# Reciprocal roots on GpSimd and one key split for both head pairs in a fused two-branch attention layer

## The chip, the cores and the metric

One core of one Trainium2 chip runs the kernel. The metric is the device time of one execution in microseconds. The core has five engines with a queue of instructions each: TensorE (PE, with its weight loads PEld beside it), VectorE (DVE), ScalarE (ACT), GpSimd (POOL) and SyncE (SP), which only issues DMAs here. An engine starts its instructions strictly in the order of its queue; semaphores order the engines among each other.

## The reference

Two request groups of 2048 tokens (`x_prompt`, `x_sample`), 1024 wide, pass one encoder layer with shared weights:

```python
h = rms_norm(x, norm_w)
q_a, k_a, v_a, g_a, q_b, k_b, v_b, g_b = split(h @ w_in)       # 512|128|128|512 and 4 x 512
q_a = partial_rope(rms_norm(q_a, q_norm_a)); k_a likewise      # per head of 64
o_a = windowed_gqa_sink(q_a, k_a, v_a, sink_a) * silu(g_a)     # 8 q heads, 2 kv heads, +-128 tokens
q_b = rms_norm(q_b, q_norm_b); k_b = rms_norm(k_b, k_norm_b)
o_b = neighbourhood_attn(q_b, k_b, v_b, rpb_b) * silu(g_b)     # 8 heads, 8 x 16 window on a 32 x 64 grid
x = x + concat(o_a, o_b) @ w_out
x = x + (p @ w_ple) * sigmoid(x @ w_ple_gate)
rms_norm(v, g) = v * rsqrt(mean(v * v) + 1e-6) * g
```

Every `rms_norm` needs a reciprocal root: one for each token, one for each head of q and of k of each token. The scores of a head are products of a normalized query and a normalized key, times `q_norm * k_norm / 8`, a factor for each of the 64 dimensions; it does not matter for the result on which of the two it is put.

## The kernel before

**Arithmetic.** Matrix products in float32 are made of three products of parts: a value is split into a high part (a copy rounded to the matmul's type, `fp32r`) and a low part (the value minus the high part), and high x high, high x low and low x high are summed. The high part is mostly a copy on ScalarE, the low part a subtraction on VectorE behind it (on GpSimd for the input x). So a tile's `project` (the helper that yields one matmul after another) is 8 x 3 = 24 matmuls of 128x128 by 512 columns (256 for `pk`).

**Stages.** `emit` writes the whole program, tile by tile, a tile being 128 tokens. The *start* (0 to about 50 us) loads and splits the first weights. The *first stage* (to about 745 us) handles branch A: 2 x 16 tiles, for each tile the projections `pk` (keys and values), `pq` and `pg` (`proj_a`), and the attention of the tile before (`unit_a`, twice, one for each kv head). The *second stage* (about 800 to 1870 us) handles branch B: two halves of four heads each, 2 x 16 tiles in each half, so 64 tiles, with the projections `pqk` and `pvg` (`proj_b`) and the attention (`unit_b`). Between the halves the weights are changed (about 1240 to 1275 us). The *last stage* (from about 1900 us) multiplies by `w_out` and the gate weights; there is no root and no key of branch B in it.

**What sets the order.** TensorE's order is fixed by hand: `mm` and `tr` (L211, L215) go through `pinned`, which ties each matmul or transpose to the one before. The tables `PLAN_A` and `PLAN_B` say at which point of the running projection which piece of an attention unit (`sc` scores, `pt` transposed exponentials, `po` output, `fin` the end of the unit, `prep` the split of the next queries) is emitted. On the other engines a scheduler sorts the instructions; those wrapped in `P` or `keep_in_program_order` keep the order of the program among themselves. Tile pools with few buffers (for example `bufs=2` for `kt`, 3 for `p_t`) tie an instruction to the last reader of the buffer.

**The root.** `rsqrt` (L135 to L145) makes y = 1/sqrt(v) on VectorE: an integer shift (L138), a subtraction from the constant 0x5F3759DF (L140), and three Newton steps of three instructions (L143 to L145): 11 instructions on a tile of 128 rows by n. It is called
- in `roots()` of `proj_a` with n = 3 (two heads of k and the token), once for each tile of the first stage; the scaled keys `kt` and their partial rotation on GpSimd (`rope`, L451 to L454) follow, and later `keys_a`, which splits the transposed keys into `ks_a` (L415, L418);
- at the end of `pq` in `proj_a` with n = 8 (eight heads of q); the multiply to `q` (L492) and a `rope` follow;
- in `proj_b` with n = 8 (four heads of q and four of k): `vrb` (L673) is the mean square, `yb` the root, and L679 multiplies it into `kb` (keys) and `qg` (queries);
- in `stats_b` with n = 16, twice, for the tokens of the second stage.

**Keys and queries of the second stage.** `keys_b` (L636) transposes the keys `kb` of a tile into the PSUM tile `pktb` (heads in pairs i, the two heads e of a pair in the two halves of the partitions) and splits them into `ks_b`: for each i and e one scaled copy on ScalarE (L645) and one scaled subtraction on VectorE (L646), 64 partitions by 128 elements, written in a scattered order (row of the grid, column). `wk[:, 1:2]`, the factor `q_norm * k_norm / 8`, is the scale. `prep_b` (L709) transposes the queries into `pqtb` and splits them without a scale: for each e a copy on ScalarE (L718), a subtraction on VectorE (L719), and a copy on GpSimd to the other half of the partitions (L721).

**Around it.** `softmax` (L227) is one VectorE instruction that adds the mask or bias to the scores and gives the row's maximum `mx`; `exps` negates the maximum (`nm`, L238 or L241), makes the exponentials on ScalarE (`s`, L243), and the denominators (L252 to L254); `pr` (L605) is the low part of the transposed exponentials of branch A; `otb` (L791) and `o_tb` (L798) are the unit's output; `split_w` (L157 to L164) splits a weight (`wx`, `wa`, `wb`); `split` (L307, L308) splits the input x.

Of the kernel before, what the change touches and what calls it, by code (L numbers as in the profile page):

```python
# [10 lines left out]

F32 = mybir.dt.float32
F32R = mybir.dt.float32r
I32 = mybir.dt.int32
AF = mybir.ActivationFunctionType
ALU = mybir.AluOpType
AX = mybir.AxisListType
# [3 lines left out]
NT = SEQ // 128  # L21
# [77 lines left out]
def emit(ctx, tc, io):  # L99
    nc = tc.nc  # L100
# [31 lines left out]
    ob_d = [dram.tile([4, 128, 4, 4, 128], F32, tag=f"ob_d{s}", name=f"ob_d{s}") for s in range(2)]  # L132
    ms_d = dram.tile([2 * SEQ], F32, tag="ms_d", name="ms_d")

    def rsqrt(pool, v, y, n, tag):  # L135
        i2 = pool.tile([128, n], I32, tag=tag + "i", name=tag + "i")
        a = pool.tile([128, n], F32, tag=tag + "a", name=tag + "a")
        nc.vector.tensor_scalar(out=i2, in0=v.bitcast(I32), scalar1=1, scalar2=None,  # L138
                                op0=ALU.logical_shift_right)
        nc.vector.tensor_scalar(out=y.bitcast(I32), in0=i2, scalar1=-1, scalar2=0x5F3759DF,  # L140
                                op0=ALU.mult, op1=ALU.add)
        for _ in range(3):
            nc.vector.scalar_tensor_tensor(out=a, in0=y, scalar=-0.5, in1=y, op0=ALU.mult, op1=ALU.mult)  # L143
            nc.vector.tensor_tensor(out=a, in0=a, in1=v, op=ALU.mult)
            nc.vector.scalar_tensor_tensor(out=y, in0=a, scalar=1.5, in1=y, op0=ALU.add, op1=ALU.mult)  # L145

    copies = []

# [272 lines left out]
    def proj_a(f):  # L421
# [35 lines left out]
        def roots():  # L457

            P(nc.vector.tensor_scalar(out=vr[:, 8:10], in0=ssq[:, 8:10], scalar1=1.0 / HD, scalar2=ee,
                                      op0=ALU.mult, op1=ALU.add))  # L460
            nc.vector.tensor_scalar(out=vr[:, 10:11], in0=ms, scalar1=EPS, scalar2=None, op0=ALU.add)
            rsqrt(ap, vr[:, 8:11], y[:, 8:11], 3, "rqk")
            nc.vector.tensor_scalar_mul(y[:, 11:12], y[:, 10:11], 0.5)
            nc.vector.tensor_tensor(out=kt[:, 0:2, :], in0=pk[:, 0:128].rearrange("p (h d) -> p h d", d=HD),
                                    in1=y[:, 8:10].unsqueeze(2).broadcast_to([128, 2, HD]), op=ALU.mult)
            rope(kt[:, 0:2, :], 2, 1)
# [4 lines left out]
        for i, c in enumerate(project(pq, xr, lambda k, b: w_q[k][:, b, :], 215)):  # L471
# [11 lines left out]
            if i == ka:  # L483
# [3 lines left out]
        nc.vector.tensor_reduce(out=ssq[:, 0:8], in_=sq.rearrange("p (h d) -> p h d", d=HD), op=ALU.add, axis=AX.X)  # L487
        nc.vector.tensor_scalar(out=vr[:, 0:8], in0=ssq[:, 0:8], scalar1=1.0 / HD, scalar2=ee,
                                op0=ALU.mult, op1=ALU.add)
        rsqrt(ap, vr[:, 0:8], y[:, 0:8], 8, "rqa")  # L490
        q = ap.tile([128, 8, HD], F32, tag="qg", name="q", bufs=6)
        nc.vector.tensor_tensor(out=q, in0=pq.rearrange("p (h d) -> p h d", d=HD),  # L492
                                in1=y[:, 0:8].unsqueeze(2).broadcast_to([128, 8, HD]), op=ALU.mult)
# [63 lines left out]
    def stats_b(s):  # L557
        c = slice(NT * s, NT * s + NT)
        tc.keep_in_program_order(nc.vector.tensor_scalar(out=ep_b[:, c], in0=ms_b[:, c], scalar1=EPS,
                                                         scalar2=EPS * EPS, op0=ALU.mult, op1=ALU.add))  # L560
        nc.vector.tensor_scalar(out=ms_b[:, c], in0=ms_b[:, c], scalar1=EPS, scalar2=None, op0=ALU.add)
        rsqrt(ap, ms_b[:, c], rs_b[:, c], NT, "rsb")
        nc.vector.tensor_scalar_mul(hr_b[:, c], rs_b[:, c], 0.5)

    qrest = {}
# [70 lines left out]
    def keys_b(kt, b, cb):  # L636
        pkt = ptile([128, 2, 16, 8], "ms", "pktb")
        for i in range(2):
            tr(pkt[:, i].rearrange("p c r -> p (c r)"), kt[:, 2 * i:2 * i + 2, :].rearrange("p h d -> p (h d)"))
        for i in range(2):  # L640
            for e in range(2):
                a, z = 64 * e, 64 - 64 * e
                hi, lo = (ks_b[i][p:p + 64, 8 * b:8 * b + 8, e, 16 * cb:16 * cb + 16].rearrange("p r c -> p c r")
                          for p in (a, z))
                nc.scalar.activation(hi, pkt[a:a + 64, i], AF.Copy, scale=wk[a:a + 64, 1:2])  # L645
                nc.vector.scalar_tensor_tensor(out=lo, in0=pkt[a:a + 64, i], scalar=wk[a:a + 64, 1:2],  # L646
                                               in1=hi.bitcast(F32), op0=ALU.mult, op1=ALU.subtract)

    def proj_b(f):
        half, st = divmod(f - 2 * NT, 2 * NT)  # L650
        s, j = divmod(st, NT)
        b, cb = divmod(j, 4)
        if f < 2 * NT + 8:
            regroup_next()
        if not ks_b:
            ks_b.extend(big([128, 32, 2, 64], F32R, f"ks_b{i}") for i in range(2))
        w_qk, w_vg = w_b[half]
        xr = xt.pop(f)
        pk = ptile([128, 512], "pj", "pqk")
        for i, c in enumerate(project(pk, xr, lambda k, b: ready("wa", k, w_qk)[:, b, :], 215)):  # L660
            at = i + 24 if f in last else i
            if i == PD and f == 2 * NT + 9:
                stats_b(1)
            if at in HX:
                split(f + 1, HX[at])
            yield c
        sq = ap.tile([128, 512], F32, tag="sq", name="sqb", bufs=2)
        nc.scalar.activation(sq, pk, AF.Square)
        ssq = ap.tile([128, 8], F32, tag="ssq", name="ssqb", bufs=3)
        nc.vector.tensor_reduce(out=ssq, in_=sq.rearrange("p (h d) -> p h d", d=HD), op=ALU.add, axis=AX.X)  # L670
        vr = ap.tile([128, 8], F32, tag="vr", name="vrb", bufs=2)
        y = ap.tile([128, 8], F32, tag="y", name="yb", bufs=4)
        nc.vector.tensor_scalar(out=vr, in0=ssq, scalar1=1.0 / HD, scalar2=ep_b[:, st:st + 1],  # L673
                                op0=ALU.mult, op1=ALU.add)
        rsqrt(ap, vr, y, 8, "rqb")
        qg = ap.tile([128, 2, 4, HD], F32, tag="qg", name="qg", bufs=6)
        kt = ap.tile([128, 4, HD], F32, tag="kt", name="kb", bufs=2)
        for dst, c in ((kt, 4), (qg[:, 0], 0)):
            nc.vector.tensor_tensor(out=dst, in0=pk[:, 64 * c:64 * c + 256].rearrange("p (h d) -> p h d", d=HD),  # L679
                                    in1=y[:, c:c + 4].unsqueeze(2).broadcast_to([128, 4, HD]), op=ALU.mult)  # L680
        yield 0, False
        pv = ptile([128, 512], "pj", "pvg")
        for i, c in enumerate(project(pv, xr, lambda k, b: ready("wb", k, w_vg)[:, b, :], 215)):
            if i + 24 in HX and f not in last:
                split(f + 1, HX[i + 24])
            yield c
            if i == (KB if f not in last else 10):
                if f < 2 * NT + 2:
                    pending.append((kt, b, cb))
                else:  # L690
                    keys_b(kt, b, cb)
        v = ap.tile([128, 4, 2, HD], F32R, tag="sq", name="vb", bufs=2)
        vp = pv[:, 0:256].rearrange("p (h d) -> p h d", d=HD)
        nc.scalar.activation(v[:, :, 0, :], vp, AF.Copy, scale=rs_b[:, st:st + 1])
        nc.vector.scalar_tensor_tensor(out=v[:, :, 1, :], in0=vp, scalar=rs_b[:, st:st + 1],
                                       in1=v[:, :, 0, :].bitcast(F32), op0=ALU.mult, op1=ALU.subtract)
        for w, (c0, ncol) in COL_WIN.items():
            lo, hi = max(c0, 16 * cb), min(c0 + ncol, 16 * cb + 16)
            if lo < hi:
                nc.sync.dma_start(v_d[half, s, w][8 * b:8 * b + 8, lo - c0:hi - c0].rearrange("r c h a d -> c r (h a d)"),  # L700
                                  v[8 * (lo - 16 * cb):8 * (hi - 16 * cb)].bitcast(F32).rearrange("p h a d -> p (h a d)"))
        gs = qg[:, 1].rearrange("p h d -> p (h d)")
        nc.scalar.activation(gs, pv[:, 256:512], AF.Tanh, scale=hr_b[:, st:st + 1])
        nc.vector.scalar_tensor_tensor(out=gs, in0=gs, scalar=1.0, in1=pv[:, 256:512], op0=ALU.add, op1=ALU.mult)
        held[f] = qg[:, 0], gs
        next(combining, None)
        yield 0, False

    def prep_b(f):  # L709
# [5 lines left out]
        q1, q2 = [q1[:, e] for e in range(2)], [q2s[f % 2][:, e, :256] for e in range(2)]  # L715
        for e in range(2):
            a, z = 64 * e, 64 - 64 * e
            nc.scalar.copy(q1[e][a:a + 64], pqt[a:a + 64])  # L718
            nc.vector.tensor_tensor(out=q2[e][a:a + 64], in0=pqt[a:a + 64], in1=q1[e][a:a + 64].bitcast(F32),  # L719
                                    op=ALU.subtract)  # L720
            nc.gpsimd.tensor_copy(q1[e][z:z + 64], q1[e][a:a + 64])  # L721
        return q1, q2

# [2 lines left out]
    def unit_b(f):  # L726
# [25 lines left out]
        def sc(h):  # L752
            ps = ptile([128, 512], "sc", "scb")
            for j, q in enumerate(qs[f]):
                mm(ps[:, :n].rearrange("p (r c) -> p r c", c=ncol), q[h % 2][:, 128 * (h // 2):128 * (h // 2) + 128],
                   ks_b[h // 2][:, r0:r0 + nr, h % 2, c0:c0 + ncol], j == 0, j == 1)
            softmax(h, ps, n, bias[:, h, :n], sm)
            if h == 3:
                got["ex"] = exps(sm, n, hr_b[:, st:st + 1], gs)
# [490 lines left out]
```

## Time and profile before

| what | value |
|---|---|
| runs | 2526.88, 2527.05, 2529.97 us (median 2527.05) |
| profiled execution | 2525.68 us; its span in the trace 2523.8 us |
| mean clock granted to TensorE | 0.996 of full speed |
| instructions | 41360 |
| busy PE, DVE, ACT, POOL | 2478.9, 1948.5, 1445.0, 582.5 us |
| DMA | 405.40 MB, mean 161 GB/s |
| chain that ended last | PE 86%, DVE 6%, DMA 3%, ACT 3% of the span |

The span is the time from the first to the last recorded instruction of the profiled execution; the execution's own time is somewhat longer. The busy time of an engine is the sum over its instructions; a matmul's end is modelled, and a weight load (PEld) runs beside the matmuls. The rows in the prediction come from these views: the page's first line and its busy line; a table by stretches (stretch, its length, then busy time with the number of instructions for PE, PEld, VectorE, ScalarE and GpSimd, then TensorE's granted clock, the mean busy share of the DMA engines and GB/s); groups of instructions (line, engine, operation, output <- inputs, shape, count | busy time in us, mean ns of one | idle time ahead of them and who ended it); a list of waits (who waits <- who ended the wait: sum in us, how many, the longest); and the timeline (start in us, duration in us, engine, line, operation, output <- inputs, shape, and in brackets a wait with its length and who ended it).

### The profile page before, as it was taken

To read this page: it belongs to the slowest core of one execution; us is meant where nothing else is said; L and a number is where in the kernel's file an instruction comes from. 1 tells how busy PE (TensorE), PEld (TensorE's weight loads), DVE (VectorE), ACT (ScalarE), POOL (GpSimd) and SP (SyncE) were. 2 spreads that over 40 slices of the span, in tenths; PEclk is the share of its full clock that TensorE was granted. 3 is DMA by queue.
4 is the path that set the end of the run, shared out by engine and by line. 5 is a ranking of instruction groups with operands and counts; after the bars stand their busy time and mean duration, and the time that the engine had idled before them with its cause. 6 is when DMAs were issued, how large, how long until landed. Compare 5 with 4: busy or idle time off the path is not lost.

```text
span 2523.8 us, 41360 instructions
## 1 busy us (share of the span) xinstructions
PE 2478.9 (98%) x12912; PEld 2090.0 (83%) x12912; DVE 1948.5 (77%) x5860; ACT 1445.0 (57%) x3469; POOL 582.5 (23%) x873
## 2 busy tenths in 40 slices
PE   8999999999989999999999999999999999999998
PEld 7888888888877888888788888888787888888887
DVE  7888888888887777787888777787746655687776
ACT  6666666666665566666666666666864222354433
POOL 3333233323323333333333333332110000000000
PEclk9999999999999999999999999999999999999999
DMA  5333332211143555555755655455867455756764
GB/s 200 98 102 109 108 88 95 64 53 62 57 101 121 167 171 177 183 166 167 235 160 180 191 160 168 147 158 185 267 230 265 160 181 171 266 176 221 235 228 154
DMA packets 236044, 405.40 MB, mean 161 GB/s; under 512 B 30864, under 2 KB 85264, under 8 KB 230416
## 3 DMA queue, kind: packets, MB, share of 16 engines
q1 hardware_dynamic: 235824, 402.75, 50.0%
q8 instruction: 103, 1.69, 0.3%
q14 instruction: 117, 0.96, 0.1%
HBM read 297.79 MB, written 122.70 MB: 167 GB/s over the span
## 4 chain that ended last, share of the span: by engine, by line
PE 86%; DVE 6%; DMA 3%; ACT 3%; issue 1%; POOL 0%; SPq 0%; DVEq 0%; ACTq 0%; POOLq 0%
PE pqk L212 13%; PE pvg L212 13%; PE acca L1082 12%; PE accc L1082 9%; PE pq L212 6%; PE pg L212 6%; PE scb L212 3%; PE ptb L215 3%; PE pob L212 3%; PE sc L212 3%; PE pk L212 3%; PE po L212 3%; PE pt L215 3%; PE pple L212 3%; ACT s L243 1%
## 5 line engine op out<-in xcount | busy, mean ns | idle before, releaser
L243 ACT ACTIVATE s<-s,nm 128x384 f32<-128x384 f32 (+4 forms) x512 | 307.3, 601 | 341.9 <-DVE nm L238 213.9
L212 PE MATMUL pvg<-wb,xr 128*128 128x512 f32 x1536 | 462.0, 408 | 0.0
L212 PE MATMUL pqk<-wa,xr 128*128 128x512 f32 x1536 | 444.7, 412 | 0.0
L212 PEld LDWEIGHTS pqk<-wa,xr 128*128 128x128 f32 x1536 | 267.7, 190 | 37.7
L212 PEld LDWEIGHTS pvg<-wb,xr 128*128 128x128 f32 x1536 | 268.4, 190 | 31.5
L308 POOL TENSOR_TENSOR xr<-stx,xr 128x512 fp32r<-128x512 f32 x190 | 245.1, 1297 | 187.0 <-ACT xr L307 180.4
L1064 ACT CAST opd<-raw 128x512 fp32r<-128x512 f32 x224 | 131.2, 619 | 261.8 <-PE acca L1082 112.8
L1065 DVE TENSOR_TENSOR opd<-raw,opd 128x512 fp32r<-128x512 f32 x224 | 146.3, 685 | 111.8 <-ACT opd L1064 111.8
L212 PE MATMUL pg<-wb,xr 128*128 128x512 f32 x768 | 231.8, 409 | 0.0
L212 PE MATMUL pq<-wa,xr 128*128 128x512 f32 x768 | 219.9, 400 | 2.2 <-DVE wa L160 1.6
L1082 PE MATMUL accc<-opd,wb 128*128 128x512 f32 x768 | 177.0, 389 | 1.9 <-DVE r L1126 1.9
L1082 PE MATMUL acca<-opd,wa 128*128 128x512 f32 x768 | 175.9, 389 | 0.4 <-DVE opd L1065 0.4
L1082 PE MATMUL acca<-opd,s 128*128 128x512 f32 x768 | 175.8, 389 | 0.2 <-DVE opd L1065 0.2
L798 POOL TENSOR_TENSOR o_tb<-otb 128x256 f32<-128x256 f32 x64 | 48.1, 751 | 547.2 <-DVE otb L791 466.8
L1082 PEld LDWEIGHTS accc<-opd,wb 128*128 128x128 f32 x768 | 144.1, 188 | 32.2 <-DVE r L1126 2.3
L1082 PEld LDWEIGHTS acca<-opd,wa 128*128 128x128 f32 x768 | 144.0, 188 | 30.9 <-DVE opd L1065 0.9
L1082 PEld LDWEIGHTS acca<-opd,s 128*128 128x128 f32 x768 | 144.0, 188 | 30.7 <-DVE opd L1065 0.9
L212 PEld LDWEIGHTS pq<-wa,xr 128*128 128x128 f32 x768 | 139.1, 188 | 25.5 <-DVE wa L160 3.3
L212 PEld LDWEIGHTS pob<-p_t,vw 128*128 128x128 f32 (+2 forms) x832 | 133.0, 190 | 30.9 <-DVE p_t L772 6.4
L227 DVE CUSTOM_DVE_ANT_0 s<-scb,bias 128x288 f32<-128x288 f32 (+3 forms) x256 | 141.3, 553 | 18.8 <-PE scb L212 15.8
L212 PEld LDWEIGHTS pg<-wb,xr 128*128 128x128 f32 x768 | 137.8, 189 | 20.4
L646 DVE SCALAR_TENSOR_TENSOR ks_b<-pktb,wk,ks_b 64x128 fp32r<-64x128 f32 x256 | 115.1, 450 | 43.9 <-ACT ks_b L645 33.4
(170 smaller groups left out, 5256.0 us busy)
## 6 DMA issues: line engine op xcount, KB each, us to landing
stx<-x_b SPq DMA_DIRECT2D x128, 256.0 KB
vw<-v_d SPq DMA_DIRECT2D x112, 256.0 KB
stx<-x_a SPq DMA_DIRECT2D x64, 256.0 KB
stn<-x_n SPq DMA_DIRECT2D x64, 256.0 KB
v_d<-vb SPq DMA_DIRECT2D x64, 256.0 KB
ple_d<-ev SPq DMA_DIRECT2D x64, 256.0 KB
xres<-x_r SPq DMA_DIRECT2D x64, 256.0 KB
x_d<-r SPq DMA_DIRECT2D x64, 256.0 KB
```

The lines of the kernel that those rows point to most:

```text
L212: pinned(nc.tensor.matmul(out, lhsT, rhs, start=start, stop=stop))
L215: pinned(nc.tensor.transpose(out, in_, eye))
L227: nc.vector.tensor_tensor_reduce(out=s[:, :n], in0=ps[:, :n], in1=bias, scale=1.0, scalar=-3.0e38, op0=ALU.add, op1=ALU.max, accum_out=sm[ ...
L243: ex = nc.scalar.activation(ss[i][:, :n], ss[i][:, :n], AF.Exp, bias=nm[:, i:i + 1], accum_out=den[:, i:i + 1])
L308: low.tensor_tensor(out=lo, in0=raw, in1=hi.bitcast(F32), op=ALU.subtract)
L646: nc.vector.scalar_tensor_tensor(out=lo, in0=pkt[a:a + 64, i], scalar=wk[a:a + 64, 1:2], in1=hi.bitcast(F32), op0=ALU.mult, op1=ALU.subtract)
L798: nc.gpsimd.tensor_tensor(out=o_t, in0=got["ot"][:, :, 0], in1=got["ot"][:, :, 1], op=ALU.add)
L1064: P(nc.scalar.copy(hi, v))
L1065: P(nc.vector.tensor_tensor(out=lo, in0=v, in1=hi.bitcast(F32), op=ALU.subtract))
L1082: pinned(nc.tensor.matmul(ps, w[k][:, a, c:c + 128], o[:, b], start=i in (0, 1, 4) and k == 0 and j == 0, stop=k == 3 and j == 2, skip_gro ...
```

## The change

`rsqrt` becomes one GpSimd instruction: v to the power of a constant tile that holds -0.5, on the same 128 rows by n. The eleven VectorE instructions and their two scratch tiles go. In `keys_b` the loop over the head pairs i goes: `ks_b` is indexed by the half of the partitions e first and by the pair i inside, so that one copy and one subtraction, 64 partitions by 256 elements, cover both pairs. The scale `wk` leaves the keys; the queries' split in `prep_b` gets it instead, with as many instructions as before. `unit_b` reads `ks_b` by the new indices.

```diff
-    def rsqrt(pool, v, y, n, tag):
-        i2 = pool.tile([128, n], I32, tag=tag + "i", name=tag + "i")
-        a = pool.tile([128, n], F32, tag=tag + "a", name=tag + "a")
-        nc.vector.tensor_scalar(out=i2, in0=v.bitcast(I32), scalar1=1, scalar2=None,
-                                op0=ALU.logical_shift_right)
-        nc.vector.tensor_scalar(out=y.bitcast(I32), in0=i2, scalar1=-1, scalar2=0x5F3759DF,
-                                op0=ALU.mult, op1=ALU.add)
-        for _ in range(3):
-            nc.vector.scalar_tensor_tensor(out=a, in0=y, scalar=-0.5, in1=y, op0=ALU.mult, op1=ALU.mult)
-            nc.vector.tensor_tensor(out=a, in0=a, in1=v, op=ALU.mult)
-            nc.vector.scalar_tensor_tensor(out=y, in0=a, scalar=1.5, in1=y, op0=ALU.add, op1=ALU.mult)
+    power = cp.tile([128, 1], F32, tag="power", name="power")
+    nc.vector.memset(power, -0.5)
+
+    def rsqrt(v, y, n):
+
+        nc.gpsimd.tensor_tensor(out=y, in0=v, in1=power.broadcast_to([128, n]), op=ALU.pow)
...
-        for i in range(2):
-            for e in range(2):
-                a, z = 64 * e, 64 - 64 * e
-                hi, lo = (ks_b[i][p:p + 64, 8 * b:8 * b + 8, e, 16 * cb:16 * cb + 16].rearrange("p r c -> p c r")
-                          for p in (a, z))
-                nc.scalar.activation(hi, pkt[a:a + 64, i], AF.Copy, scale=wk[a:a + 64, 1:2])
-                nc.vector.scalar_tensor_tensor(out=lo, in0=pkt[a:a + 64, i], scalar=wk[a:a + 64, 1:2],
-                                               in1=hi.bitcast(F32), op0=ALU.mult, op1=ALU.subtract)
+        for e in range(2):
+            a, z = 64 * e, 64 - 64 * e
+            hi, lo = (ks_b[e][p:p + 64, 8 * b:8 * b + 8, :, 16 * cb:16 * cb + 16].rearrange("p r i c -> p i c r")
+                      for p in (a, z))
+            nc.scalar.copy(hi, pkt[a:a + 64])
+            nc.vector.tensor_tensor(out=lo, in0=pkt[a:a + 64], in1=hi.bitcast(F32), op=ALU.subtract)
...
-            nc.scalar.copy(q1[e][a:a + 64], pqt[a:a + 64])
-            nc.vector.tensor_tensor(out=q2[e][a:a + 64], in0=pqt[a:a + 64], in1=q1[e][a:a + 64].bitcast(F32),
-                                    op=ALU.subtract)
+            nc.scalar.activation(q1[e][a:a + 64], pqt[a:a + 64], AF.Copy, scale=wk[a:a + 64, 1:2])
+            nc.vector.scalar_tensor_tensor(out=q2[e][a:a + 64], in0=pqt[a:a + 64], scalar=wk[a:a + 64, 1:2],
+                                           in1=q1[e][a:a + 64].bitcast(F32), op0=ALU.mult, op1=ALU.subtract)
...
-                   ks_b[h // 2][:, r0:r0 + nr, h % 2, c0:c0 + ncol], j == 0, j == 1)
+                   ks_b[h % 2][:, r0:r0 + nr, h // 2, c0:c0 + ncol], j == 0, j == 1)
```

The four calls of `rsqrt` lose their pool and tag. Seen by engines: TensorE's order is the same, instruction for instruction. VectorE has 1430 root instructions and 128 key splits less, ScalarE 128 key copies less, GpSimd 130 powers more (32 of 128x3, 96 of 128x8, 2 of 128x16). On VectorE the scheduler sets some instructions in another order around the roots: in the second stage one of the four masked sums now comes between `vrb` and `kb` in most tiles. The order in which SyncE issues the DMAs is nearly the same.

More of the change, by code (lines that the diff above doesn't have):

```diff
@@ L13 @@
 F32R = mybir.dt.float32r
-I32 = mybir.dt.int32
 AF = mybir.ActivationFunctionType
@@ L461, in roots @@
             nc.vector.tensor_scalar(out=vr[:, 10:11], in0=ms, scalar1=EPS, scalar2=None, op0=ALU.add)
-            rsqrt(ap, vr[:, 8:11], y[:, 8:11], 3, "rqk")
+            rsqrt(vr[:, 8:11], y[:, 8:11], 3)
             nc.vector.tensor_scalar_mul(y[:, 11:12], y[:, 10:11], 0.5)
@@ L489, in proj_a @@
                                 op0=ALU.mult, op1=ALU.add)
-        rsqrt(ap, vr[:, 0:8], y[:, 0:8], 8, "rqa")
+        rsqrt(vr[:, 0:8], y[:, 0:8], 8)
         q = ap.tile([128, 8, HD], F32, tag="qg", name="q", bufs=6)
@@ L561, in stats_b @@
         nc.vector.tensor_scalar(out=ms_b[:, c], in0=ms_b[:, c], scalar1=EPS, scalar2=None, op0=ALU.add)
-        rsqrt(ap, ms_b[:, c], rs_b[:, c], NT, "rsb")
+        rsqrt(ms_b[:, c], rs_b[:, c], NT)
         nc.vector.tensor_scalar_mul(hr_b[:, c], rs_b[:, c], 0.5)
@@ L655, in proj_b @@
         if not ks_b:
-            ks_b.extend(big([128, 32, 2, 64], F32R, f"ks_b{i}") for i in range(2))
+            ks_b.extend(big([128, 32, 2, 64], F32R, f"ks_b{e}") for e in range(2))
         w_qk, w_vg = w_b[half]
@@ L674, in proj_b @@
                                 op0=ALU.mult, op1=ALU.add)
-        rsqrt(ap, vr, y, 8, "rqb")
+        rsqrt(vr, y, 8)
         qg = ap.tile([128, 2, 4, HD], F32, tag="qg", name="qg", bufs=6)
```

## The prediction

> **What bounds the kernel now.** First the page: the span and the busy shares.
>
> ```profile
> span 2523.8 us, 41360 instructions
> PE 2478.9 (98%) x12912; PEld 2090.0 (83%) x12912; DVE 1948.5 (77%) x5860; ACT 1445.0 (57%) x3469; POOL 582.5 (23%) x873
> ```
>
> PE is busy for 2478.9 of 2523.8 us. So a change that leaves PE's instructions alone can win at most the 45 us in which PE idles, plus what PE loses to a lower clock. Where is that? The busy time by stretch (columns: stretch, length, then busy time of PE, PEld, DVE, ACT, POOL, then PE's granted clock):
>
> ```profile
> 0.00:50.00 50.00, 40.30 (x196) 33.55 (x197) 37.10 (x125) 30.19 (x65) 16.58 (x35) 1.00 0.63 213
> 50.00:700.00 650.00, 647.82 (x3741) 567.55 (x3740) 561.67 (x2166) 437.75 (x1187) 207.50 (x397) 1.00 0.27 85
> 700.00:800.00 100.00, 90.98 (x444) 73.25 (x443) 83.09 (x265) 65.38 (x159) 28.09 (x39) 0.95 0.43 115
> 800.00:1200.00 400.00, 399.10 (x2137) 334.51 (x2136) 308.40 (x1007) 242.20 (x590) 134.76 (x158) 1.00 0.54 168
> 1200.00:1300.00 100.00, 93.22 (x489) 77.05 (x489) 81.97 (x234) 66.80 (x154) 32.22 (x38) 0.97 0.67 209
> 1750.00:1900.00 150.00, 144.22 (x759) 118.94 (x758) 90.39 (x239) 105.36 (x238) 19.26 (x31) 1.00 0.76 249
> ```
>
> In the steady stretches (50 to 700, 800 to 1200) PE idles 3 us in 1050. It idles 9.7 us in the first 50 us, 9.0 where the first stage ends (700 to 800), 6.8 where the second stage changes its weights (1200 to 1300) and 5.8 before the last stage; the clock takes about 5 us more in the third of these rows (100 x 0.05) and 3 in the fifth. The last stage, from 1900 on, has no root and no key of the second stage; its share is out of reach. Who ends PE's waits:
>
> ```profile
> PE pk L212 <- ACT wx L159: 6.2, 2, 5.9
> PE sc L212 <- DVE mx L227: 4.6, 5, 2.5
> PE pob L212 <- DVE q L719: 4.4, 2, 3.3
> PE ptb L215 <- ACT s L243: 3.0, 3, 1.4
> PE sc L212 <- DVE pr L605: 2.8, 3, 1.8
> ```
>
> The 6.2 us are the first weights. The rows of VectorE here sum to 11.8 us, and shorter ones follow. That, and part of the clock's 8 us, is what a lighter VectorE can give.
>
> **Part 1, the roots.** Removed from VectorE:
>
> ```profile
> L144 DVE TENSOR_TENSOR rqba<-rqba,vrb 128x8 f32<-128x8 f32 x192 | 32.0, 166 | 5.2
> L143 DVE SCALAR_TENSOR_TENSOR rqba<-yb 128x8 f32<-128x8 f32 x192 | 31.9, 166 | 4.9
> L145 DVE SCALAR_TENSOR_TENSOR yb<-rqba,yb 128x8 f32<-128x8 f32 x192 | 31.9, 166 | 5.2
> ```
>
> 192 is 3 Newton steps for 64 roots of the second stage; with the two integer steps ahead of them (L138, L140) a root is 11 instructions. The first stage has 2 roots in each of 32 tiles, and 2 more serve the tokens: 130 x 11 = 1430 instructions, at 0.166 us some 237 us busy. Alone in the queue they follow each other by 0.20 us (1209.99 and 1210.19 below), so a root is 2.2 us of VectorE.
>
> Added: 130 powers on GpSimd, 128 rows by 3, 8 or 16. No row shows a power. The nearest rows:
>
> ```profile
> L451 POOL TENSOR_TENSOR r<-q,tab 128x128 f32<-128x128 f32 x32 | 14.8, 463 | 248.3 <-DVE q L492 243.7 <-DVE den L252 4.6
> ...
> L453 POOL TENSOR_TENSOR r<-kt,tab 128x16 f32<-128x16 f32 x32 | 7.2, 224 | 0.0
> ```
>
> A multiply of 128x16 takes 0.224 us there and each further element 0.002, so nearly all of it is fixed cost: 0.22 us is the lower end for a power (below that nothing can lie). For the upper end I replace the power by the eleven passes it replaces, each at that row: 11 x 0.224 = 2.5 us; and I keep in mind that a function done without the lanes' parallelism would be longer still. I take 0.8 us for eight elements and 0.6 for three, nearer to the lower end, because the element's share is so small.
>
> A root's result now crosses to GpSimd and back. How much room is there? One tile of the second stage, VectorE first, then PE:
>
> ```profile
> 1208.99 0.23 DVE L673 TENSOR_SCALAR vrb<-ssqb,ep_b 128x8 f32<-128x8 f32 x1
> 1209.13 0.53 DVE L227 CUSTOM_DVE_ANT_0 s<-scb,bias 128x360 f32<-128x360 f32 x1
> ...
> 1209.99 0.17 DVE L143 SCALAR_TENSOR_TENSOR rqba<-yb 128x8 f32<-128x8 f32 x1
> 1210.19 0.17 DVE L144 TENSOR_TENSOR rqba<-rqba,vrb 128x8 f32<-128x8 f32 x1
> ...
> 1212.13 0.42 DVE L679 TENSOR_TENSOR kb<-pqk,yb 128x256 f32<-128x256 f32 x1
> ```
> ```profile
> 1214.71 0.49 PE L215 MATMUL ptb<-rowwise,s 128*120 128x128 f32 x3
> ```
>
> In the changed order VectorE's queue has vrb, one of the masked sums (L227, with the row's maximum), kb, the last masked sum, nm. GpSimd has nothing queued before the power that is late (its next work, o_tb, follows the ot of VectorE some 5 us later), so kb starts at about 1209.3 + 0.8 = 1210.1 instead of 1212.13. In the first stage kt and its half stand right behind the root and VectorE waits the whole 0.6 us plus 0.2 of handing over, but 2.2 fall away; the second root there has a subtraction of pr (L605) before its use. So a tile of the first stage frees about 4.4 - 0.8 - 0.2 = 3.4 us of VectorE, one of the second some 2.
>
> In the steady stretches this is worth nothing: PE covers it. It counts where VectorE is late. The two longest such waits stand at the end of the first stage:
>
> ```profile
> 726.64 0.62 PE L212 MATMUL sc<-ks_a,q 128*128 128x384 f32 x2 [1.75 <-DVE pr L605]
> ...
> 730.08 1.01 PE L212 MATMUL sc<-ks_a,q 128*128 128x384 f32 x2 [2.52 <-DVE mx L227]
> ```
>
> From 705 on VectorE works without a break up to them, and two roots lie in that row of work. Up to 3.4 us earlier, but the weight splits between are tied to ScalarE and DMA: I take 1.5 of these 4.3 us, and 1 us of the slower clock behind them, 2.5. At 747 to 753 one root is spread between masked sums and weights; of the other waits for mx (4.6 - 2.5 = 2.1 in all) I take 1. At 1268 to 1274 a root stands ahead of nm, and PE waits for s (longest 1.4): 1.3. Small ones elsewhere: 0.6.
>
> On the other side stand two places. At the start the sixth and seventh weight of the q projection are now queued behind both tiles' first roots:
>
> ```profile
> 22.20 0.75 DVE L160 SCALAR_TENSOR_TENSOR wa<-ws,nw,wa 128x512 fp32r<-128x512 f32 x1
> ...
> 23.01 2.17 PE L212 MATMUL pq<-wa,xr 128*128 128x512 f32 x8 [1.62 <-DVE wa L160]
> ```
>
> Eight steps of the first root (8 x 0.2 = 1.6 us) that stood ahead of the first weight shown go; eight short instructions of both tiles, about as long, come ahead of it, and two powers: 22.2 + 2 x 0.6 = 23.4. PE loses 1.2 us, and the other roots of these two tiles, no longer on VectorE, give about as much back before PE's first transposes of q. I count 0. And at 786 to 789, where the first stage ends, kb's wait stands ahead of the second ot whose end PE waits for: +0.8, the power's length.
>
> **Part 2, the keys.** Four splits of 64x128 become two of 64x256 on each engine:
>
> ```profile
> L646 DVE SCALAR_TENSOR_TENSOR ks_b<-pktb,wk,ks_b 64x128 fp32r<-64x128 f32 x256 | 115.1, 450 | 43.9 <-ACT ks_b L645 33.4
> ...
> L719 DVE TENSOR_TENSOR q<-pqtb,q1b 64x256 fp32r<-64x256 f32 x128 | 53.6, 419 | 3.4 <-ACT q1b L718 1.2
> ...
> L418 DVE SCALAR_TENSOR_TENSOR ks_a<-pkt,wk,ks_a 64x128 fp32r<-64x128 f32 x64 | 22.4, 350 | 4.3 <-ACT ks_a L415 2.3
> ```
>
> The scattered write costs 0.10 us per 128 elements more than a plain one (450 against 350), a plain 64x256 takes 419, so a new split is 0.62 (at most 2 x 0.45, at least 0.419). VectorE frees 128 x (0.90 - 0.62) = 36 us and ScalarE about as much, again hidden by PE in the steady stretches. It helps where weights are split at the same time (1240 to 1258, 1770 to 1785): 0.3 us each, 0.6. The scale moves to the queries, whose two instructions keep their shape: nothing.
>
> **The sum.** -2.5 - 1 - 1.3 - 0.6 - 0.6 + 0.8 + 0 = -5.2 us. The profiled execution took 2525.68 us (span 2523.8 and 1.9 around it); the median of the runs is 2527.05, 1.4 more. 2525.7 - 5.2 = 2520.5, say **2521 us**.
>
> **The rivals.**
>
> *Slow power (slower).*
>
> ```profile
> L243 ACT ACTIVATE s<-s,nm 128x384 f32<-128x384 f32 (+4 forms) x512 | 307.3, 601 | 341.9 <-DVE nm L238 213.9
> ```
>
> VectorE's queue stops at kb. The first ptb at 1214.71 needs an exponential on ScalarE (601 ns, and some 0.3 of handing over), so nm is due at about 1213.8; it comes at 1210.4 plus the power (1209.3, kb 0.42, a masked sum 0.53, some 0.15 between). So from a power of 3.4 us on, every tile of the second stage pays: 64 x (power - 3.4). At 5 us that is +102, 2628. For it: no row shows the function, and 2.5 us is only a stand-in. Against: 3.4 us is 15 times the row of 128x16.
>
> *PE hides all.* The late places are late for the weight splits and for ScalarE, not for roots; the gains shrink to 1 or 2 us and the two losses stay: 2524 to 2530. For it: 98% busy.
>
> *A costly first power.* Both first roots stand ahead of a weight PE waits for, so a first power that is longer by some us costs that much: 2521 + 6 = 2527 for 6 us. The Trainium skill (GPSIMD Engine Reference, 2.1 Instruction dispatch) has about 6 us for the first call of a freshly loaded kernel; no row of this trace shows such a gap.
>
> *The clock keeps up.* The rows 700 to 800 and 1200 to 1300 alone fall to 0.95 and 0.97, and both have PE's longest waits. If waits cut short leave PE at full clock, all 5 + 3 = 8 us of slower work go, not the 1 counted: 2520.5 - 7 = 2513.5. For it: no other row falls below 1.00, though the start and 1750 to 1900 idle too. Against: the sum takes 2.5 and 1.3 us of the 9.0 and 6.8 of idleness in these rows; most stays. The Trainium skill (TensorE: Matmul & The Clock Gate, Part 1: The HAM clock gate) says that a window of about 3.4 us of idleness halves PE's clock until it has been busy as long; by that rule a wait cut somewhat shorter could be enough.
>
> **How the numbers follow.** A measurement of this kernel can tell about 0.2%, 5 us. Forecast 0.45 (2516 to 2524: 0.35 below 2522.0, 0.10 within); the clock keeps up 0.05, faster; PE hides all 0.18, within; costly first power 0.08 (0.06 within, 0.02 slower); slow power 0.24, slower. Faster 0.40, within 0.34, slower 0.26. The range 2512 to 2550 takes in powers from 0.22 us to some 3.6 us; it leaves out about 0.02 below and 0.16 above.
>
> **What would show it.** Right: VectorE's busy time falls by some 270 us, GpSimd's rises by about 100, PE's waits for mx, pr and s in 700 to 800 and 1200 to 1300 shrink, the clock there rises. Wrong: a power over 2.5 us; waits of kb or kt for GpSimd that exceed 2 us; new waits of PE for kb, s or wa; a split of keys over 0.9 us.

## The result and the profile after

The changed kernel takes 2598.79 us (median of 4 runs, 2596.41 to 2603.3) against 2527.06 us before (4 runs, 2526.88 to 2529.97): 1.0283 times the time, 95% interval 1.0265 to 1.0301, or 72 us more. The forecast was 2521 us, faster. The execution profiled is the longest of the four, 2603.3 us with a span of 2601.4; its granted clock is 0.993, that of the others 0.996 or 0.997.

The page of the changed kernel, its first line and its busy line:

```profile
span 2601.4 us, 39713 instructions
PE 2509.4 (96%) x12912; PEld 2088.6 (80%) x12912; DVE 1731.5 (67%) x4303; ACT 1413.0 (54%) x3341; POOL 773.5 (30%) x1003
```

VectorE lost 217 us of work (1948.5 before), GpSimd gained 191, and the span grew by 77.6. No engine beside TensorE is near its full load. TensorE's idle time grew from 44.9 to 92.0 us; the rest of the 77.6 stands in its busy time, 30.5 us more for the same instructions. The powers, by shape (groups of instructions of GpSimd; the 32 of 128x8 for q, in the first stage, take 1.65 us each as well):

```profile
L139 POOL TENSOR_TENSOR yb<-vrb,power 128x8 f32<-128x8 f32 x64 | 106.0, 1656 | 211.9 <-DVE vrb L665 204.5 <-DMA raw<-w_out 2.8 <-DMA stx<-x_b 2.5
L139 POOL TENSOR_TENSOR y<-vr,power 128x3 f32<-128x3 f32 x32 | 27.5, 860 | 63.2 <-DVE vr L453 63.2
L139 POOL TENSOR_TENSOR rs_b<-ms_b,power 128x16 f32<-128x16 f32 x2 | 5.8, 2906 | 0.3 <-DVE ms_b L555 0.3
```

0.86 us for 3 elements, 1.66 for 8, 2.91 for 16: about 0.39 us and 0.157 for each element of a row. So a power is well short of the 3.4 us that the prediction gave as the point from which it hurts. What TensorE waits for now (us in total, times, longest):

```profile
PE sc L206 <- DVE mx L221: 26.1, 29, 2.0
PE pob L206 <- DVE p_t L764: 18.1, 55, 0.8
PE pob L206 <- DVE q L711: 7.3, 8, 3.5
```

Two rows carry it: sc for mx was 4.6 us in 5 waits before, pob for p_t 2.4 in 4. They are not long waits at the edges but short ones in nearly every tile, in the stretches where TensorE did not wait before.

TensorE runs the same instructions in the same order in both kernels, so each matmul can be set beside itself. How much later it starts than before, stage by stage, worked out from the two traces (starts are compared, so this takes in idle and busy time):

| stretch of before's span, us | later by | where |
|---|---|---|
| 0 to 50 | 6.2 | weights of the q projection, first scores |
| 50 to 700 (first stage) | 31.0 | 28.9 ahead of sc, 2.1 at the first power of 128x16 |
| 700 to 830 | 1.7 | 1.7 won ahead of sc, 1.6 lost at the first pktb, the rest among pt, pvg and pg |
| 830 to 1200 (second stage) | 15.6 | 14.0 ahead of and among pob |
| 1200 to 1350 (weight change) | 4.3 | 5.4 at pob, about 1 won |
| 1350 to 1750 (second stage) | 16.9 | 16.9 at pob |
| rest | 0.9 | |

**One tile of the first stage.** The timeline before (start, duration, engine, line, instruction), VectorE and TensorE:

```profile
283.87 0.22 DVE L488 TENSOR_SCALAR vr<-ssq,ee 128x8 f32<-128x8 f32 x1
...
284.60 0.16 DVE L138 TENSOR_SCALAR rqai<-vr 128x8 int32<-128x8 int32 x1
284.67 0.55 DVE L227 CUSTOM_DVE_ANT_0 s<-sc,mask 128x384 f32<-128x384 f32 x1
...
284.91 0.86 PE L212 MATMUL sc<-ks_a,q 128*128 128x384 f32 x4
...
285.14 0.17 DVE L140 TENSOR_SCALAR y<-rqai 128x8 int32<-128x8 int32 x1
...
285.95 0.51 PE L212 MATMUL sc<-ks_a,q 128*128 128x384 f32 x2
...
289.13 0.69 DVE L492 TENSOR_TENSOR q<-pq,y 128x512 f32<-128x512 f32 x1
```

The root of the queries was a chain of short steps, and between its steps stand the masked sums of the next scores: the first one starts 0.80 us after vr, and q comes last, 5.26 us after it. The same place in the changed kernel:

```profile
300.95 0.22 DVE L482 TENSOR_SCALAR vr<-ssq,ee 128x8 f32<-128x8 f32 x1
...
301.26 1.65 POOL L139 TENSOR_TENSOR y<-vr,power 128x8 f32<-128x8 f32 x1 [3.58 <-DVE vr L482]
...
302.10 0.86 PE L206 MATMUL sc<-ks_a,q 128*128 128x384 f32 x4
...
302.94 0.69 DVE L486 TENSOR_TENSOR q<-pq,y 128x512 f32<-128x512 f32 x1 [1.17 <-POOL y L139]
...
303.55 0.55 DVE L221 CUSTOM_DVE_ANT_0 s<-sc,mask 128x384 f32<-128x384 f32 x1
...
304.16 0.61 PE L206 MATMUL sc<-ks_a,q 128*128 128x384 f32 x2 [0.86 <-DVE mx L221]
```

Here q stands ahead of the first masked sum. VectorE waits 1.17 us for the power, multiplies for 0.69, and only then comes the masked sum, 2.60 us after vr. Scores go to three PSUM buffers, so the fourth sc needs the first one read: it starts 2.06 us after the second and third, which stand in one row, not 1.04. That is 1.02 us lost, in nearly every tile.

**One tile of the second stage.** Before (VectorE), then after (VectorE, GpSimd, ScalarE, TensorE):

```profile
1048.79 0.23 DVE L673 TENSOR_SCALAR vrb<-ssqb,ep_b 128x8 f32<-128x8 f32 x1
...
1050.30 0.55 DVE L227 CUSTOM_DVE_ANT_0 s<-scb,bias 128x384 f32<-128x384 f32 x1
...
1050.89 0.17 DVE L238 TENSOR_SCALAR nm<-mx 128x4 f32<-128x4 f32 x1
...
1051.98 0.42 DVE L679 TENSOR_TENSOR kb<-pqk,yb 128x256 f32<-128x256 f32 x1
```
```profile
1096.89 0.23 DVE L665 TENSOR_SCALAR vrb<-ssqb,ep_b 128x8 f32<-128x8 f32 x1
...
1098.88 0.42 DVE L671 TENSOR_TENSOR kb<-pqk,yb 128x256 f32<-128x256 f32 x1 [1.29 <-POOL yb L139]
1099.22 0.55 DVE L221 CUSTOM_DVE_ANT_0 s<-scb,bias 128x384 f32<-128x384 f32 x1
...
1099.81 0.17 DVE L232 TENSOR_SCALAR nm<-mx 128x4 f32<-128x4 f32 x1
...
1100.75 0.58 ACT L782 COPY otb<-pob 64x512 f32<-64x512 f32 x1
...
1103.16 0.45 ACT L710 ACTIVATE q1b<-pqtb,wk 64x256 fp32r<-64x256 f32 x1
...
1103.75 0.39 POOL L713 CAST q1b<-q1b 64x256 fp32r<-64x256 f32 x1 [0.89 <-ACT q1b L710]
...
1104.22 0.61 POOL L250 TENSOR_TENSOR g<-qg,rd 128x256 f32<-128x256 f32 x1
...
1104.66 0.41 ACT L763 CAST p_t<-ptb 128x304 fp32r<-128x304 f32 x1
1104.87 0.42 DVE L671 TENSOR_TENSOR qg<-pqk,yb 128x256 f32<-128x256 f32 x1 [0.74 <-POOL g L250]
...
1105.85 0.47 DVE L764 TENSOR_TENSOR p_t<-ptb,p_t 128x304 fp32r<-128x304 f32 x1
...
1106.38 0.56 PE L206 MATMUL pob<-p_t,vw 128*128 128x256 f32 x3 [0.24 <-DVE p_t L764]
```

Counted from vrb, kb comes earlier than before (1.99 us instead of 3.19), as the prediction had it. But the last masked sum and nm are now behind it: nm comes at 2.92 instead of 2.10. From nm on everything is in a row over three engines. On ScalarE there are an exponential, the copy otb, three more exponentials and the first copy of the queries (q1b); on GpSimd the second copy of q1b and, behind it in the queue, g; on VectorE qg, which waits 0.74 us for g, the low part of the queries and the low part of the first p_t. That one ends 0.06 us before pob starts, 0.24 us late. ScalarE's part of p_t, done at 1105.07, is not what it waits for. From nm to the end of this low part it is 6.53 us in the median tile. Of the 36.8 us that the second stage loses between 830 and 1750, 26.5 stand at the first pob of a tile and 9.9 at the second. kb, which came earlier, is not needed until the keys are transposed, 4 us later.

### The profile page after: what moved, and what is told of

It reads as the page before. It is cut to its first block, busy times and chain, and to the rows that moved or that the text cites. A ratio compares the mean times of both kernels' runs of the same rounds, so it can differ in the third digit from the quotient of the medians.

```text
span 2601.4 us, 39713 instructions
## 1 busy us (share of the span) xinstructions
PE 2509.4 (96%) x12912; PEld 2088.6 (80%) x12912; DVE 1731.5 (67%) x4303; ACT 1413.0 (54%) x3341; POOL 773.5 (30%) x1003
## 4 chain that ended last, share of the span: by engine, by line
PE 35%; DVE 9%; issue 7%; ACT 6%; POOL 6%; DMA 5%; SPq 0%; POOLq 0%; DVEq 0%; ACTq 0%
PE acca L1074 12%; PE accc L1074 9%; PE pvg L206 4%; PE pqk L206 4%; PE pple L206 3%; POOL yb L139 2%; DMA bias<-bias 2%; ACT s L237 2%; POOL xr L302 2%; PE scb L206 2%; DMA ob_d<-o_tb 2%; PE pob L206 2%; ACT ks_b L638 1%; DVE ks_b L639 1%; DVE p_t L764 1%
## 5 line engine op out<-in xcount | busy, mean ns | idle before, releaser
L139 POOL TENSOR_TENSOR yb<-vrb,power 128x8 f32<-128x8 f32 x64 | 106.0, 1656 | 211.9 <-DVE vrb L665 204.5
L206 PEld LDWEIGHTS pq<-wa,xr 128*128 128x128 f32 x768 | 141.9, 192 | 28.9 <-DVE wa L154 5.8
L206 PE MATMUL pob<-p_t,vw 128*128 128x256 f32 (+7 forms) x832 | 132.8, 273 | 26.4 <-DVE p_t L764 18.1
L783 DVE TENSOR_TENSOR otb<-pob,otb 64x512 f32<-64x512 f32 x128 | 88.1, 688 | 100.3 <-ACT otb L782 97.4
```

What stands on the lines that cost most here:

```text
L139: nc.gpsimd.tensor_tensor(out=y, in0=v, in1=power.broadcast_to([128, n]), op=ALU.pow)
L206: pinned(nc.tensor.matmul(out, lhsT, rhs, start=start, stop=stop))
L783: nc.vector.tensor_tensor(out=ot[a:a + 64], in0=pq[a:a + 64], in1=ot[a:a + 64], op=ALU.add)
```

## The experiments

Three theories. **Queue**: VectorE takes its instructions in order, and the order puts the user of a power (q, kb) ahead of masked sums that could run; their lateness is the price. **Length**: the power is on the path of its own data, q and k reach TensorE too late. **Keys**: the second part makes ScalarE and VectorE late in the second stage.

**e1_roots: the powers alone.** The kernel before with the new `rsqrt`; `keys_b`, `prep_b` and `unit_b` as before.

> The kernel before with the powers alone; the keys are split as before. Queue theory (the wait for the power stands on VectorE ahead of masked sums that TensorE needs): nearly all of the +72 us comes from this part, 2588 to 2600 us, with the same gap of about 1.0 us per first-stage tile ahead of sc. Keys theory (the doubled split and the scaled queries make VectorE and ScalarE late for p_t in the second stage, where 37 of the 77 us arise): 2555 to 2570 us. Length theory (the power's 1.65 us on the data's path): also about 2590.

Measured 2590.04 us, 1.0248 (1.0233 to 1.0264), as the queue and the length theory both have it.

**e2_keys: the keys alone.** The changed kernel with VectorE's steps back in `rsqrt`.

> The kernel before with the new key split and the scale on the queries alone; the roots stay on VectorE. Queue theory: 2522 to 2529 us, no change beyond what a measurement tells. Keys theory: over 2545 us, with TensorE waiting for p_t in nearly every tile of the second stage.

Measured 2531.58 us, 1.0019 (1.001 to 1.0029): 3.6 us slower beside 2527.96 of the kernel before on the same chip. So 62 of the 72 us are the powers'. The keys theory falls as the main cause, yet the part is not free, and the time lies above the 2522 to 2529 us that the queue theory expected: 4 us alone, and about 9 between e1_roots and the changed kernel.

**e3_late: the users behind nm.** Same powers, same lengths, another place in VectorE's queue:

```diff
-        nc.vector.tensor_tensor(out=q, ...)          # at the end of pq
-        rope(q, 8, 0)
+        def queries():
+            behind(nc.vector.tensor_tensor(out=q, ...))   # ordered after the last nm
+            rope(q, 8, 0)
...
+            if i == 14 and f > 1:                    # in pg's loop
+                queries()
...
+            if i == 10:                              # in pvg's loop: kb and qg, each behind(...)
+                scaled()
```

> The changed kernel, but what uses the root of eight is put behind the negated maximum on VectorE: in the first stage the multiply to q, in the second the multiplies to kb and qg. The powers and their length stay. Queue theory: the steady stages lose their gaps and only the start (+5), the two powers of 128x16 (+4) and a few odd places stay: 2525 to 2540 us. Length theory: q and kb come no earlier than in the changed kernel, so nothing is won, 2595 to 2610 us.

Measured 2525.9 us, 0.9995 (0.9986 to 1.0005): all of the 72 us are gone. The first stage's queue in e3_late (VectorE), and what TensorE still waits for:

```profile
289.67 0.22 DVE L491 TENSOR_SCALAR vr<-ssq,ee 128x8 f32<-128x8 f32 x1
...
290.56 0.56 DVE L221 CUSTOM_DVE_ANT_0 s<-sc,mask 128x384 f32<-128x384 f32 x1
...
293.95 0.69 DVE L497 TENSOR_TENSOR q<-pq,y 128x512 f32<-128x512 f32 x1
```
```profile
PE sc L206 <- DVE mx L221: 3.3, 4, 1.9
...
PE pob L206 <- DVE p_t L785: 1.6, 2, 0.8
```

q comes 4.28 us after vr, 2.29 later than in the changed kernel (5.26 after vr in the kernel before), and nothing waits for it: the length theory falls. The masked sum is back at 0.89 us.

**e4_short: no power at all.** `op=ALU.pow` becomes `op=ALU.mult`, the order is the changed kernel's.

> The changed kernel with each power replaced by one GpSimd multiply on the same tiles (the roots are left out: v times -0.5 stands in their place, so the output is not the reference's). Order, waits and crossings stay, only the length falls, from 1.65 us to about 0.25 for eight elements. Queue theory with the power's length as the price: the wait ahead of the masked sums falls to 0.2 to 0.4 us, 2520 to 2532 us. If the crossing to GpSimd and back, or the order itself, is what costs: 2555 us or more.

Measured 2521.18 us, 0.9971 (0.9962 to 0.998), the multiply 0.20 us. VectorE and ScalarE have exactly the order of the changed kernel, so the order hurts only by the length of the wait at its head. That the time is the forecast's 2521 is luck: the forecast took powers of 0.8 and 0.6 us and a start that loses nothing, and here the start loses 2.7.

**e5_late_oldkeys: e3_late with the keys as before** (the same edit on e1_roots).

> The powers with their users put behind the negated maximum, as in e3_late, and the keys split as before. If the key part costs 3 to 4 us wherever VectorE's and ScalarE's work is a little late (as in e2_keys): 2521 to 2523 us, below e3_late's 2525.9. If the earlier negated maximum of e3_late hides it: 2525 to 2528.

Measured 2527.03 us, 0.9994 (0.9985 to 1.0003). With nm early the key part makes no difference that shows.

**e6_start: e3_late, with start and token roots moved.**

```diff
-        if f < 2:
-            roots()
...
-            if i == PC and f > 1:
+            if i == PC:
                 roots()
...
-        nc.vector.tensor_scalar_mul(hr_b[:, c], rs_b[:, c], 0.5)   # in stats_b
+            if i == PD + 1 and f == NT + 10:         # one tile later; likewise for the second
+                halves_b(0)
```

> e3_late, with the first roots of the first two tiles behind the weights of the q projection, and the halving of the token roots (hr_b) one tile behind its power of 128x16. Queue theory: the 5 us of the start and the 2 us at the first power of 128x16 go, 2518 to 2521 us, faster than before by 0.25 to 0.4%. If the start is late for another reason (the power's own length ahead of the first transposes): 2523 to 2527.

Measured 2524.94 us, 0.9991 (0.9983 to 1.0): a miss. The weights of q came in time, but the keys of the first tiles, whose roots moved behind them, were late for pkt and the first scores (3.8 us at 50 us, 5.4 in e3_late); and hr_b was put directly behind its power again, because only its place in the program had moved.

**e7_slack: before, with a pass more ahead of nm.**

```diff
+            for extra in [nc.vector.tensor_tensor(out=idle, in0=ss[3][:, :256], in1=ss[3][:, :256], op=ALU.add)]:
+                tc.add_manual_dep(ins.ins, extra.ins.name, ...)    # nm behind it
```

> The kernel before with one more pass of 128x256 on VectorE (about 0.4 us, its result is not used) between the last masked sum and the negated maximum of each tile of the second stage; roots and keys as before. The prediction had the negated maximum due some 3 us later than it comes; by that nothing changes, 2526 to 2530. By the changed kernel's trace (0.8 us later there, and TensorE waits 0.4 to 0.7 us for p_t in each tile) the chain behind it has a slack of some 0.3 us: 64 x 0.1 to 0.4, 2534 to 2555.

Measured 2529.48 us, 1.0011 (1.0002 to 1.002), no more than a trace of a cost, but not a clean test: the scheduler knew of the pass and set ScalarE's copy otb ahead of the exponentials, which takes its 0.6 us out of the row behind nm; and the 0.4 us of the pass lie within the room of 0.6 found below. e9_wait and e10_wait4 keep ScalarE's order but for a few tiles.

**e8_start_oldkeys: e6_start with the keys as before.**

> e6_start with the keys split as before: the powers alone, all their users placed behind what TensorE waits for. If the key part costs by itself: 2 to 4 us below e6_start, 2514 to 2518. If it is hidden: equal to e6_start within 1.5 us.

Measured 2524.43 us, 0.9986 (0.9978 to 0.9995): equal to e6_start, faster than before by a little.

**e9_wait and e10_wait4: the wait without kb, and a longer one.**

```diff
         rsqrt(vr, y, 8)
+        z = y                                        # e10_wait4: a second power, rsqrt(vr[:, :4], z, 4)
+        nc.vector.tensor_scalar_mul(idle, z[:, 0:1], 1.0)
```

> e3_late (users behind the negated maximum), with one element-wide reader of the second stage's root put back between the third and the last masked sum on VectorE, where kb stood in the changed kernel; kb stays behind. Only the wait returns, not kb. The negated maximum then comes about 0.2 us earlier than in the changed kernel (4.45 us after the tile's first pvg matmul, not 4.67) and 0.85 later than in e3_late. Queue theory, with the changed kernel's 0.6 us lost per tile at 4.67: it decides from about 4.1, so some 0.35 us per tile, 64 x 0.35 = 22 us, 2540 to 2555. If kb's own place, and not the late negated maximum, was the cause: 2524 to 2530.

> As e9_wait, but the reader waits for a second power of 128x4 behind the first (about 1.0 us more on GpSimd; its result is not used). The negated maximum comes at about 5.45 us. Queue theory: 64 x (5.45 - 4.1) = 86 us, 2600 to 2620. If VectorE's wait is not what TensorE waits for: as e9_wait.

Measured 2554.67 us, 1.011 (1.0095 to 1.0126), and 2615.29 us, 1.0349 (1.0335 to 1.0363). A tile of each, VectorE:

```profile
1058.83 0.23 DVE L683 TENSOR_SCALAR vrb<-ssqb,ep_b 128x8 f32<-128x8 f32 x1
...
1060.81 0.15 DVE L687 TENSOR_SCALAR idle<-yb 128x1 f32<-128x1 f32 x1 [1.29 <-POOL yb L139]
...
1061.47 0.17 DVE L241 TENSOR_SCALAR nm<-mx 128x4 f32<-128x4 f32 x1
```
```profile
1056.87 0.23 DVE L683 TENSOR_SCALAR vrb<-ssqb,ep_b 128x8 f32<-128x8 f32 x1
...
1059.83 0.15 DVE L688 TENSOR_SCALAR idle<-zb 128x1 f32<-128x1 f32 x1 [2.37 <-POOL zb L139]
...
1060.39 0.17 DVE L241 TENSOR_SCALAR nm<-mx 128x4 f32<-128x4 f32 x1
```

One instruction of 128x1 that only waits costs 28.8 us over e3_late, 0.45 per tile; a wait that is longer by 1.0 us costs 89.4, 1.40 per tile. The two tiles above differ in the width of their scores. Over all tiles nm comes 2.63 us after vrb in e9_wait and 3.61 in e10_wait4 (medians), so a later nm costs about its full lateness (0.95 for 0.98). Carried back at that rate, the cost begins at about 2.63 - 0.45 = 2.2 us after vrb, an estimate. The kernel before stands at 2.10, the changed one at 2.90.

The traces show the room at the first pob directly. In the kernel before, the low part of the first p_t ends 0.6 us ahead of the pob that reads it (median; 0.2 to 1.0 in most tiles); in the changed kernel, e9_wait and e10_wait4 it is 0.05 to 0.06, for there TensorE waits for it. By this nm had until about 2.10 + 0.6 = 2.7 us, also an estimate, and one that counts the first pob alone. So nm is due between 2.2 and 2.7 us after vrb.

**e11_mixed and e12_mixed_keys: powers only where they are covered.** e5_late_oldkeys and e3_late, with VectorE's steps (`steps`, the old `rsqrt`) for the first two tiles and the two roots of 128x16:

```diff
-            rsqrt(ap, vr[:, 8:11], y[:, 8:11], 3, "rqk")
+            (steps if f < 2 else rsqrt)(ap, vr[:, 8:11], y[:, 8:11], 3, "rqk")
...
-        rsqrt(ap, ms_b[:, c], rs_b[:, c], NT, "rsb")
+        steps(ap, ms_b[:, c], rs_b[:, c], NT, "rsb")
```

> Powers for the 30 later tiles of the first stage and for the second stage, their users behind the negated maximum; VectorE's steps for the first two tiles and for the two roots of 128x16; keys as before. In e8_start_oldkeys the start still cost 3.6 us and the power of 128x16 2.1 us (0.9 in the second stage). Queue theory: these 6 us go, 2518 to 2520, faster than before by 0.25 to 0.35%. If the start is late for something else, 2523 to 2525.

> e11_mixed with the new key split and the scale on the queries. If the key part is hidden wherever the negated maximum is early (as e3_late beside e5_late_oldkeys and e6_start beside e8_start_oldkeys suggest): equal to e11_mixed's 2518.9 within 1.5 us. If its longer splits cost by themselves, as in e2_keys: 2522 to 2524.

Measured 2518.87 us, 0.9965 (0.9952 to 0.9977), and 2516.4 us, 0.9954 (0.994 to 0.9967). Both are faster than both kernels; the key part and 124 of the 130 powers, with their users in other places, win 0.46%. e12_mixed_keys is 2.5 us below e11_mixed, where at most 1.5 apart was expected; the two were not run together and their intervals overlap, so whether the key part adds to it is open. One of TensorE's waits in e12_mixed_keys:

```profile
PE sc L219 <- DVE mx L234: 1.4, 3, 0.9
```

The 4.6 us of sc for mx of the kernel before are down to 1.4; the longest of them, 2.5 us at the end of the first stage, is one of those on which the forecast was built.

## Why the prediction was wrong

**What bounds the kernel: right.** TensorE leaves 45 us, and the gain lies in the few places where VectorE is late. e12_mixed_keys wins 11 us, more than the 5.2 of the sum, most of it there: matmul by matmul, 3.8 us between 700 and 830 and 2.5 at the weight change, of 8.6 in the two profiled executions.

**The power's price: too low, within its bounds.** 0.8 and 0.6 us were taken, 1.66 and 0.86 measured; the upper end of 2.5 held for eight elements. The element's share was read from a multiply (0.002 us); a power has 0.157. The powers of 128x16 (2.91 us) were not priced. But e3_late has the same powers and loses nothing, so this size alone does not make the 72 us. Nor would the order alone have made them: with a power of 0.8 us, nm would have come 1.27 + 0.8 = 2.1 us after vrb, in time, and the first stage would have lost 1.02 - 0.85 = 0.17 us per tile (estimates from the rows above).

**"In the steady stretches this is worth nothing: PE covers it": the step that failed.** It took away VectorE's work and asked when kb and q come. It did not ask what stands behind them. So it called the whole range of powers up to 2.5 us harmless here, and the measured 1.66 lies in that range. In the second stage the prediction named the instructions in the queue, "one of the masked sums, kb, the last masked sum, nm", and then set nm's due time by the first transposed exponential, 4.8 us after vrb. Between nm and the first pob lies the whole row over ScalarE, GpSimd and VectorE; with it counted, nm was due 2.2 to 2.7 us after vrb. In the changed kernel nm comes at 1.27 us plus the power (2.92 with 1.65), so a tile pays from a power of some 0.9 to 1.4 us on, not from 3.4. The rival of the slow power had the mechanism, with the point from which it decides set 2 us or more too high.

**The first stage: not seen.** The prediction noted that pr stands between the second root and q, and counted 3.4 us per tile as freed. The masked sums, which had stood between the steps of the chain, are behind q now. The price, 1.02 us in nearly every tile, makes nearly all of the 28.9 us ahead of sc in the stretch from 50 to 700.

**The start, counted as 0: 6.2.** The two powers ahead of the sixth weight were foreseen, as a loss of 1.2 to be given back. VectorE and TensorE in the changed kernel:

```profile
22.27 0.15 DVE L457 TENSOR_SCALAR y<-y 128x1 f32<-128x1 f32 x1 [0.98 <-POOL y L139]
...
24.50 0.15 DVE L457 TENSOR_SCALAR y<-y 128x1 f32<-128x1 f32 x1 [1.16 <-POOL y L139]
...
24.77 1.40 DVE L154 SCALAR_TENSOR_TENSOR wa<-ws,nw,wa 128x512 fp32r<-128x512 f32 x2
```
```profile
25.56 1.65 PE L206 MATMUL pq<-wa,xr 128*128 128x512 f32 x3 [3.58 <-DVE wa L154]
```

The weight starts at 24.77, not 23.4: two waits of about 1.1 us, and the second root's short instructions between them. TensorE starts on it 2.55 us later than before, and only 0.7 us were given back, ahead of the first transposes of q. Most of the rest of the 6.2 is the clock: between 0 and 50 us this execution was granted 0.93 of full speed, 1.00 before, which is 50 x 0.07 = 3.5 us. What length of wait lowers it, these traces do not settle: with the old wait of 1.6 us at this place, e12_mixed_keys has 0.97 there.

The rival of a costly first power did not come: the first, at 21.37 us, takes 0.86 us like the others. The 6 us of the Trainium skill (GPSIMD Engine Reference, 2.1 Instruction dispatch), stated for the first call of a freshly loaded kernel, do not show in this program.

**The powers of 128x16: left out.** hr_b stands behind the first one and makes VectorE wait 3.02 us, and TensorE 1.94:

```profile
607.67 0.18 DVE L557 TENSOR_SCALAR hr_b<-rs_b 128x16 f32<-128x16 f32 x1 [3.02 <-POOL rs_b L139]
```
```profile
609.74 0.66 PE L209 MATMUL pt<-ident,s 128*128 128x128 f32 x4 [1.94 <-DVE ot L622]
```

**The gains at the edges: right in place.** 2.5 us were taken at the end of the first stage; ahead of sc, the changed kernel wins 2.7 between 705 and 735 and 1.7 between 700 and 830. The +0.8 at 786 to 789 was 1.6. At the weight change, 1.3 were taken; e3_late wins 2.4 there ahead of ptb.

**The keys: sizes right, "nothing" wrong.** After, and the queries' copy before:

```profile
L639 DVE TENSOR_TENSOR ks_b<-pktb,ks_b 64x256 fp32r<-64x256 f32 x128 | 79.7, 623 | 11.3 <-ACT ks_b L638 8.4
L711 DVE SCALAR_TENSOR_TENSOR q<-pqtb,wk,q1b 64x256 fp32r<-64x256 f32 x128 | 61.7, 482 | 8.6 <-ACT q1b L710 6.8
...
L710 ACT ACTIVATE q1b<-pqtb,wk 64x256 fp32r<-64x256 f32 x128 | 59.2, 462 | 48.1 <-DVE q L711 44.9 <-PE pqtb L209 3.0
```
```profile
L718 ACT CAST q1b<-pqtb 64x256 fp32r<-64x256 f32 x128 | 46.1, 360 | 47.0 <-DVE q L719 44.8 <-PE pqtb L215 2.0
```

A split takes 0.623 us; 0.62 was forecast. The scale on the queries was priced at nothing: ScalarE's copy went from 0.360 to 0.462 us, VectorE's low part from 0.419 to 0.482. Both stand in the row between nm and the first pob. From nm to the end of the first low part it is 6.35 us in e1_roots and 6.53 in the changed kernel (medians): 0.18 us, 64 times, is 11.5. By the traces the second stage loses 23.7 us in e1_roots and 36.8 in the changed kernel, and 11 of these 13 us more stand at the first pob of a tile. So the 9 us that the key part costs beside the powers come from this longer row, as far as the traces tell; no run changed the row alone.

**The clock that keeps up** is not borne out: e12_mixed_keys, with the shorter waits, has 0.98 between 700 and 800 and 0.97 between 1200 and 1300 (0.95 and 0.97 before), and over the whole execution 0.996, as before.

## What to carry to other kernels

When a chain of short instructions on an engine becomes one instruction elsewhere, ask for each of its users what stands behind it in the queue: the gaps between the chain's steps carried other work, and a wait has no gaps. Give the deadline of the first instruction behind the wait by the whole row of work up to the engine that must not stop, through every engine on the way (here six instructions of ScalarE, two of GpSimd and three of VectorE), not by the next one. Then the remedy is an order, not a shorter operation: the user of the late result goes behind what is urgent and ready, and where nothing is there to cover the wait (the start, a single large root) the old chain is the better one.

## What the runs showed of the hardware

A power on GpSimd costs by the element of a row: 0.86, 1.66 and 2.91 us for 3, 8 and 16, where a multiply in its place takes 0.20 for 3 to 8 and 0.21 for 16 (e4_short). 191 us more of GpSimd's work and some 90 short waits of TensorE left the granted clock between 50 and 700 at 0.99 and between 1350 and 1800 at 1.00. And an engine that is 67% busy can cost TensorE more than one that is 77% busy.
